# Column mean of an 8192 x 8192 float32 matrix: loads in float32 on SyncE's queue, sums in float32 in four column groups

## The chip, the cores and the metric

The kernel runs on one core of one Trainium2 chip. The metric is the device time of one execution in microseconds, taken as the median of several runs. A profiled execution gives the trace; its span runs from the first to the last instruction and is a little shorter than the time of a run.

## The reference

```python
def setup_inputs():
    return {
        "x": np.random.randn(8192, 8192).astype(np.float32),
    }

def reference(x: np.ndarray) -> np.ndarray:
    return np.mean(x, axis=0)
```

The input has 268.44 MB, all of which is read once; the output has 8192 float32 values (32 KB).

## The kernel before

**Tiling.** The 8192 rows are 64 slabs of 128 rows: a row of x lies along one SBUF partition, 8192 columns (32 KB of float32) long. Summing over the rows of a slab is a matrix product with a column of ones: `mm` (line 104) cuts a slab into 16 chunks of 512 columns, and `mm_seg` (line 90, the matmul at line 95) multiplies one chunk by `ones`, so that one output row of 512 sums is added up in PSUM over all 64 slabs. All matmuls are bf16, with a stationary operand of 128 x 1.

**Where the sums lie.** `acc` covers all eight PSUM banks. Chunks 0 to 7 are summed in partition 0, chunks 8 to 15 in partition 32, one chunk per bank; the last chunk is split into two halves of 256 columns, and its second half lies in partition 64 (`seg_psum`, line 82). These partitions decide which column group of TensorE a matmul uses.

**Loads.** Nearly all loads are issued on POOL's (GpSimd's) queue, and the transfer itself casts float32 to bf16, so half as many bytes are written to SBUF as are read:

- slab 0: its first 2048 columns come as float32 on SP's queue (`hx`, line 128) and are cast by VectorE (line 130); the rest comes over POOL (`t0`, line 136; the profile calls this buffer t_89).
- slabs 1 to 61: three slabs per transfer (line 158; 20 of them, 12.58 MB read and 6.29 MB written each), into two buffers; slab 61 comes alone (line 163). A load waits until TensorE has finished with the buffer.
- `place_orphans` (line 140): the last 8 rows of slab 62, columns 5632 to 8191, come early by a small load of their own (line 143) into the zeroed tile `xtra`, on partitions 0, 16, 32 and so on, and are added there.
- slab 62: two loads (lines 183 and 184), the second without those 8 rows.
- slab 63: pieces of 4096, 2048, 1024 and 512 columns (`b_piece`, line 200), then two of 256 (`b_cols`, line 223).

**Output.** `drain` (line 108) copies one row of 512 sums from PSUM to `res`, times 1/8192, alternately on VectorE (line 118) and ScalarE (line 116). `res` is one row on one partition, and goes out in four transfers: three on SP (lines 207, 213 and 237), one on ACT (line 240).

**Order.** Each queue runs in the order of the program. TensorE goes through the slabs in order; POOL issues loads ahead of it as far as the two slab buffers allow, and the tail's loads (lines 183 to 200), which have buffers of their own, right after the last slab load.

Of the kernel before, what the change touches and what calls it, by code (L numbers as in the profile page):

```python
# [7 lines left out]

@with_exitstack
def kernel(
# [8 lines left out]
    assert R % P == 0, "row count must be a multiple of 128"  # L21
    n_slabs = R // P
    s_last = n_slabs - 1

    MM_DT = mybir.dt.bfloat16
    CHUNK = 512
    BANKS = 8
    n_chunks = (C + CHUNK - 1) // CHUNK
    n_rows = (n_chunks + BANKS - 1) // BANKS + 1
    QROWS = (0, 32, 64, 96)  # L30
    assert n_rows <= len(QROWS)
    inv_r = 1.0 / float(R)

    SPD = int(os.environ.get("CM_SPD", "3"))
    HEADW = int(os.environ.get("CM_HEADW", "2048"))
    REB = int(os.environ.get("CM_REB", "1"))
    HEADW = min(HEADW, C)
    if HEADW % CHUNK:
        HEADW = (HEADW // CHUNK) * CHUNK

    two_slab_tail = n_slabs >= 4 and n_chunks == 16
    if not two_slab_tail or C < 2 * CHUNK:
        REB = 0
    DONOR_LO = 120
    ORPH_STEP = 16
    ORPHW = int(os.environ.get("CM_ORPHW", "2560"))
    ORPHW = min(max((ORPHW // CHUNK) * CHUNK, CHUNK), C)
    C1 = C - ORPHW

    const_pool = ctx.enter_context(tc.tile_pool(name="const", bufs=1))  # L50
    head_pool = ctx.enter_context(tc.tile_pool(name="head", bufs=1))
    slab_pool = ctx.enter_context(tc.tile_pool(name="slab", bufs=2))
    tail_pool = ctx.enter_context(tc.tile_pool(name="tail", bufs=1))
    psum_pool = ctx.enter_context(tc.tile_pool(name="acc", bufs=1, space=bass.MemoryType.PSUM))
    res_pool = ctx.enter_context(tc.tile_pool(name="res", bufs=1))

    ones_f32 = const_pool.tile([P, 1], mybir.dt.float32)
    nc.vector.memset(ones_f32, 1.0)
    ones = const_pool.tile([P, 1], MM_DT)
    nc.scalar.copy(out=ones, in_=ones_f32)  # L60

    if REB:
        xtra = tail_pool.tile([P, ORPHW], MM_DT, tag="xz")
        nc.vector.memset(xtra, 0.0)  # L64

    acc = psum_pool.tile([P, BANKS * CHUNK], mybir.dt.float32)
    res = res_pool.tile([1, C], mybir.dt.float32)

    def chunk_psum(c):
        q, b = c // BANKS, c % BANKS  # L70
        cw = min(CHUNK, C - c * CHUNK)
        return acc[QROWS[q] : QROWS[q] + 1, b * CHUNK : b * CHUNK + cw]

    FINW = CHUNK // 2

    def csegs(c):
        lo, hi = c * CHUNK, min(C, (c + 1) * CHUNK)
        if two_slab_tail and c == n_chunks - 1 and hi - lo == CHUNK:
            return ((lo, lo + FINW), (lo + FINW, hi))
        return ((lo, hi),)  # L80

    def seg_psum(c, lo, hi):
        q, b = c // BANKS, c % BANKS
        o = b * CHUNK - c * CHUNK
        if two_slab_tail and c == n_chunks - 1 and lo >= c * CHUNK + FINW:
            q += 1
            o = -(c * CHUNK + FINW)
        return acc[QROWS[q] : QROWS[q] + 1, o + lo : o + hi]

    def mm_seg(slab_ap, ordpos, c, lo, hi, base=0, prange=None):  # L90
        p0, p1 = (0, P) if prange is None else prange
        tp = None
        if prange is not None and p0 not in (0, 32, 64):
            tp = ((p0 // 32) * 32, QROWS[c // BANKS])
        nc.tensor.matmul(  # L95
            out=seg_psum(c, lo, hi),
            lhsT=ones[p0:p1, :],
            rhs=slab_ap[p0:p1, lo - base : hi - base],
            start=(ordpos == 0),
            stop=(ordpos == s_last),  # L100
            tile_position=tp,
        )

    def mm(slab_ap, ordpos, c, base=0, prange=None):
        for lo, hi in csegs(c):
            mm_seg(slab_ap, ordpos, c, lo, hi, base, prange)

    def drain(c, eng=None):
        c0 = c * CHUNK
        cw = min(CHUNK, C - c0)  # L110
        src_ap = chunk_psum(c)
        dst_ap = res[0:1, c0 : c0 + cw]
        if eng is None:
            eng = "dve" if c % 2 == 0 else "act"
        if eng == "act":
            nc.scalar.mul(out=dst_ap, in_=src_ap, mul=inv_r)  # L116
        else:
            nc.vector.tensor_scalar(  # L118
                out=dst_ap,
                in0=src_ap,  # L120
                scalar1=inv_r,
                scalar2=None,
                op0=mybir.AluOpType.mult,
            )

    if HEADW:
        hx = head_pool.tile([P, HEADW], mybir.dt.float32, tag="hx")
        nc.sync.dma_start(out=hx, in_=x[0:P, 0:HEADW])
        hxb = head_pool.tile([P, HEADW], MM_DT, tag="hxb")
        nc.vector.tensor_copy(out=hxb, in_=hx)  # L130
        for c in range(HEADW // CHUNK):
            mm(hxb, 0, c)

    if HEADW < C:
        t0 = slab_pool.tile([P, SPD * C], MM_DT, tag="slab")
        nc.gpsimd.dma_start(out=t0[:, : C - HEADW], in_=x[0:P, HEADW:C])  # L136
        for c in range(HEADW // CHUNK, n_chunks):
            mm(t0[:, : C - HEADW], 0, c, base=HEADW)

    def place_orphans():  # L140
        r0 = (n_slabs - 2) * P + DONOR_LO
        nd = P - DONOR_LO
        nc.gpsimd.dma_start(  # L143
            out=xtra.rearrange("(a b) c -> a b c", b=ORPH_STEP)[:nd, 0, :],
            in_=x[r0 : r0 + nd, C1:C],
        )
        for c in range(C1 // CHUNK, n_chunks):
            mm(xtra, 1, c, base=C1)

    bulk_end = (n_slabs - 2) if two_slab_tail else n_slabs  # L150
    s0 = 1
    first_group = True
    while s0 < bulk_end:
        ns = min(SPD, bulk_end - s0)
        slab = slab_pool.tile([P, SPD * C], MM_DT, tag="slab")
        src = x[s0 * P : (s0 + ns) * P, :]
        if ns > 1:
            nc.gpsimd.dma_start(  # L158
                out=slab[:, : ns * C].rearrange("p (k c) -> p k c", c=C),
                in_=src.rearrange("(k p) c -> p k c", p=P),  # L160
            )
        else:
            nc.gpsimd.dma_start(out=slab[:, :C], in_=src)  # L163
        for k in range(ns):
            for c in range(n_chunks):
                mm(slab[:, k * C : (k + 1) * C], s0 + k, c)
        s0 += ns
        if first_group:
            first_group = False
            if REB:  # L170
                place_orphans()

    if not two_slab_tail:
        for c in range(n_chunks):
            drain(c)
        nc.sync.dma_start(out=out[0:C], in_=res[0:1, 0:C])
        return

    sa = n_slabs - 2
    rowa = x[sa * P : (sa + 1) * P, :]  # L180
    abuf = tail_pool.tile([P, C], MM_DT, tag="ta")
    if REB:
        nc.gpsimd.dma_start(out=abuf[:, 0:C1], in_=rowa[:, 0:C1])  # L183
        nc.gpsimd.dma_start(out=abuf[0:DONOR_LO, C1:C], in_=rowa[0:DONOR_LO, C1:C])  # L184
        for c in range(n_chunks):
            if c < C1 // CHUNK:
                mm(abuf, sa, c)
            else:
                mm(abuf, sa, c, prange=(0, DONOR_LO))
    else:  # L190
        nc.gpsimd.dma_start(out=abuf, in_=rowa)
        for c in range(n_chunks):
            mm(abuf, sa, c)

    rowb = x[s_last * P : (s_last + 1) * P, :]
    bbuf = tail_pool.tile([P, C], MM_DT, tag="tb")

    def b_piece(c_lo, c_hi):
        lo, hi = c_lo * CHUNK, c_hi * CHUNK
        nc.gpsimd.dma_start(out=bbuf[:, lo:hi], in_=rowb[:, lo:hi])  # L200
        for c in range(c_lo, c_hi):
            mm(bbuf, s_last, c)

    b_piece(0, 8)
    for c in range(0, 8):
        drain(c)
    nc.sync.dma_start(out=out[0 : 8 * CHUNK], in_=res[0:1, 0 : 8 * CHUNK])

    b_piece(8, 12)
    drain(8, "dve"); drain(9, "act"); drain(10, "dve"); drain(11, "act")  # L210
    b_piece(12, 14)
    drain(12, "dve"); drain(13, "act")
    nc.sync.dma_start(out=out[8 * CHUNK : 14 * CHUNK], in_=res[0:1, 8 * CHUNK : 14 * CHUNK])
    b_piece(14, 15)
    drain(14, "dve")

    FIN = os.environ.get("CM_FIN", "act")
    lo15 = (n_chunks - 1) * CHUNK
    hi15 = min(C, lo15 + CHUNK)
    mid = lo15 + FINW  # L220

    def b_cols(lo, hi, eng):
        nc.gpsimd.dma_start(out=bbuf[:, lo:hi], in_=rowb[:, lo:hi])  # L223
        c = lo // CHUNK
        mm_seg(bbuf, s_last, c, lo, hi)
        src = seg_psum(c, lo, hi)
        dst = res[0:1, lo:hi]
        if eng == "act":
            nc.scalar.mul(out=dst, in_=src, mul=inv_r)  # L229
# [43 lines left out]
```

## Time and profile before

| | |
|---|---|
| median of 3 runs | 629.56 us (629.27 to 629.67) |
| span of the profiled execution | 627.5 us |
| DMA, mean of all engines over the span | 215 GB/s written; packets 9632, 134.91 MB |
| POOL's queue | 9472 packets, 133.70 MB (bf16) |
| SP's and ACT's queues | 152 packets, 1.08 MB |
| instruction loading | 8 packets, 0.13 MB |
| mean granted TensorE clock | 0.655 |

GB/s and the queues count the bytes that are written; the HBM row of the page counts what is read. The costliest groups of instructions (line, engine, operation, output and input, count; busy time and mean of one; idle time of the engine before them, and what ended it):

```
L95 PE MATMUL acc<-slab,ones 128*1 128x512 bf16 x1037 | 165.0, 439 | 426.3 <-DMA slab<-in_x_dram 426.3
L95 PEld LDWEIGHTS <-ones 128*1 128x1 bf16 x1094 | 63.3, 94 | 560.4 <-issue 513.4
L158 POOL DMA_DIRECT2D slab<-in_x_dram x20 | 15.3, 764 | 527.1 <-PE acc L95 527.1
L118 DVE TENSOR_SCALAR res<-acc 1x512 f32<-1x512 f32 x8 | 5.3, 678 | 613.1 <-PE acc L95 613.1
L116 ACT ACTIVATE res<-acc 1x512 f32<-1x512 f32 x7 | 3.9, 583 | 618.2 <-PE acc L95 618.2
```

An engine's idle time costs nothing where the engine is not the bound: TensorE waits 426.3 us for the slab loads, and POOL 527.1 us for TensorE to release a slab buffer.

### The profile page before, as it was taken

Reading aid. Unit: us, or ns where it says so; the run is one execution under the profiler, and the core shown is the slowest. Engines: PE = TensorE matmul, PEld = TensorE weight load, DVE = VectorE, ACT = ScalarE, POOL = GpSimd, SP = SyncE. Lnnn points to the kernel's source line nnn. Section 1 sums busy time; section 2 is a strip of 40 time slices with the busy share of each in tenths; the row PEclk is TensorE's granted clock in tenths of the full one; section 3 lists DMA queues with packets and bytes.
Section 4 is the critical chain, followed back from the end, with each engine's and each line's share of the span. In section 5 each row is a group of like instructions: output and inputs, shape, how many; then the busy total and the mean of one; then the engine's idle time right before and its main releaser. Section 6 shows DMA issues by size and latency. Waiting matters only on the chain.

```text
span 627.5 us, 2316 instructions
## 1 busy us (share of the span) xinstructions
PE 181.1 (29%) x1094; PEld 63.3 (10%) x1094; DVE 8.0 (1%) x12; ACT 5.7 (1%) x10; POOL 21.6 (3%) x35
## 2 busy tenths in 40 slices
PE   3032405040504133140405040422314050405165
PEld 0011101010101011010101010101101010101021
DVE  1000000000000000000000000000000000000003
ACT  0000000000000000000000000000000000000002
POOL 1000000000000000000000000000000000002000
PEclk9997666575757575656757575757566565757587
DMA  9999999999999999999999999999999999999997
GB/s 219 217 218 217 217 217 217 217 217 217 217 217 217 217 217 217 217 217 217 216 216 216 216 217 215 217 217 217 217 217 215 216 217 217 216 213 218 216 214 143
DMA packets 9632, 134.91 MB, mean 215 GB/s; under 512 B 532, under 2 KB 917, under 8 KB 1302
## 3 DMA queue, kind: packets, MB, share of 16 engines
q0 software_dynamic: 9472, 133.70, 100.0%
q1 hardware_dynamic: 150, 1.08, 0.5%
q8 instruction: 8, 0.13, 0.1%
q10 hardware_dynamic: 2, 0.00, 0.0%
HBM read 268.44 MB, written 0.03 MB: 428 GB/s over the span
## 4 chain that ended last, share of the span: by engine, by line
DMA 84%; PE 14%; issue 1%; POOL 0%; DVE 0%; DVEq 0%; POOLq 0%
DMA slab<-in_x_dram 77%; PE acc L95 14%; DMA bbuf<-in_x_dram 7%; DVE res L118 0%; POOL t_89 L136 0%; POOL slab L163 0%; POOL abuf L183 0%; POOL abuf L184 0%; DVEq L268 0%; POOLq L257 0%
## 5 line engine op out<-in xcount | busy, mean ns | idle before, releaser
L95 PE MATMUL acc<-slab,ones 128*1 128x512 bf16 x1037 | 165.0, 439 | 426.3 <-DMA slab<-in_x_dram 426.3
L95 PEld LDWEIGHTS <-ones 128*1 128x1 bf16 x1094 | 63.3, 94 | 560.4 <-issue 513.4
L158 POOL DMA_DIRECT2D slab<-in_x_dram x20 | 15.3, 764 | 527.1 <-PE acc L95 527.1
L118 DVE TENSOR_SCALAR res<-acc 1x512 f32<-1x512 f32 x8 | 5.3, 678 | 613.1 <-PE acc L95 613.1
L116 ACT ACTIVATE res<-acc 1x512 f32<-1x512 f32 x7 | 3.9, 583 | 618.2 <-PE acc L95 618.2
L95 PE MATMUL acc<-bbuf,ones 128*1 128x512 bf16 (+1 forms) x17 | 5.8, 599 | 3.3 <-DMA bbuf<-in_x_dram 3.3
L95 PE MATMUL acc<-abuf,ones 128*1 128x512 bf16 (+2 forms) x17 | 4.1, 517 | 2.9 <-DMA abuf<-in_x_dram 2.9
L95 PE MATMUL acc<-t_89,ones 128*1 128x512 bf16 (+1 forms) x13 | 3.4, 589 | 4.1 <-DMA t_89<-in_x_dram 4.1
L95 PE MATMUL acc<-hxb,ones 128*1 128x512 bf16 x4 | 1.9, 622 | 6.7 <-DVE hxb L130 6.7
L200 POOL DMA_DIRECT2D bbuf<-in_x_dram x4 | 2.1, 547 | 0.0
L223 POOL DMA_DIRECT2D bbuf<-in_x_dram x2 | 1.1, 532 | 26.0 <-DMA slab<-in_x_dram 26.0
L163 POOL DMA_DIRECT2D slab<-in_x_dram x1 | 0.6, 586 | 29.1 <-PE acc L95 29.1
L60 ACT ACT_TABLE_LOAD x1 | 1.3, 1283 | 0.7 <-PEq L257 0.7
L130 DVE CAST hxb<-hx 128x2048 bf16<-128x2048 f32 x1 | 1.2, 1227 | 3.2 <-DMA hx<-in_x_dram 3.2
L95 PE MATMUL acc<-xtra,ones 128*1 128x512 bf16 (+1 forms) x6 | 1.1, 343 | 0.0
L64 DVE MEMSET xtra<- 128x1280 uint32 x1 | 1.1, 1125 | 0.2 <-issue 0.2
L136 POOL DMA_DIRECT2D t_89<-in_x_dram x1 | 0.7, 669 | 0.8 <-POOLq L257 0.8
L143 POOL DMA_DIRECT2D xtra<-in_x_dram x1 | 0.6, 588 | 0.0
L184 POOL DMA_DIRECT2D abuf<-in_x_dram x1 | 0.6, 556 | 0.0
L183 POOL DMA_DIRECT2D abuf<-in_x_dram x1 | 0.6, 553 | 0.0
L231 DVE TENSOR_SCALAR res<-acc 1x256 f32<-1x256 f32 x1 | 0.4, 405 | 0.0
L229 ACT ACTIVATE res<-acc 1x256 f32<-1x256 f32 x1 | 0.4, 377 | 0.1
(6 smaller groups left out, 0.7 us busy)
## 6 DMA issues: line engine op xcount, KB each, us to landing
slab<-in_x_dram POOLq DMA_DIRECT2D x20, 6144.0 KB, 49.9
slab<-in_x_dram POOLq DMA_DIRECT2D x1, 2048.0 KB, 30.0
t_89<-in_x_dram POOLq DMA_DIRECT2D x1, 1536.0 KB, 11.4
abuf<-in_x_dram POOLq DMA_DIRECT2D x1, 1408.0 KB, 36.6
hx<-in_x_dram SPq DMA_DIRECT2D x1, 1024.0 KB, 4.7
bbuf<-in_x_dram POOLq DMA_DIRECT2D x1, 1024.0 KB, 42.9
abuf<-in_x_dram POOLq DMA_DIRECT2D x1, 600.0 KB, 38.6
bbuf<-in_x_dram POOLq DMA_DIRECT2D x1, 512.0 KB, 44.9
```

Source lines behind the costliest of these rows:

```text
L60: nc.scalar.copy(out=ones, in_=ones_f32)
L64: nc.vector.memset(xtra, 0.0)
L95: nc.tensor.matmul(out=seg_psum(c, lo, hi), lhsT=ones[p0:p1, :], rhs=slab_ap[p0:p1, lo - base : hi - base], start=(ordpos == 0), stop=(ord ...
L116: nc.scalar.mul(out=dst_ap, in_=src_ap, mul=inv_r)
L118: nc.vector.tensor_scalar(out=dst_ap, in0=src_ap, scalar1=inv_r, scalar2=None, op0=mybir.AluOpType.mult,)
L130: nc.vector.tensor_copy(out=hxb, in_=hx)
L136: nc.gpsimd.dma_start(out=t0[:, : C - HEADW], in_=x[0:P, HEADW:C])
L143: nc.gpsimd.dma_start(out=xtra.rearrange("(a b) c -> a b c", b=ORPH_STEP)[:nd, 0, :], in_=x[r0 : r0 + nd, C1:C],)
L158: nc.gpsimd.dma_start(out=slab[:, : ns * C].rearrange("p (k c) -> p k c", c=C), in_=src.rearrange("(k p) c -> p k c", p=P),)
L163: nc.gpsimd.dma_start(out=slab[:, :C], in_=src)
L200: nc.gpsimd.dma_start(out=bbuf[:, lo:hi], in_=rowb[:, lo:hi])
L223: nc.gpsimd.dma_start(out=bbuf[:, lo:hi], in_=rowb[:, lo:hi])
```

## The change

The kernel's body is written anew:

- **Loads.** All loads are plain float32 transfers on SP's queue, with no cast; POOL issues nothing. A tile is 256 rows: partition p holds rows 2p and 2p+1 of the tile, one run of 64 KB in memory. Three buffers of 64 KB per partition; 31 such tiles of 8.39 MB.
- **The last 256 rows** are the 32nd tile: first 128 rows in one transfer (32 KB per partition), then the last 128 rows in six pieces of 2048, 2048, 2048, 1024, 512 and 512 columns, each a transfer of its own.
- **Sums.** TensorE adds in float32. The columns are split into the same six pieces; each piece has one PSUM bank, and its four quarters are summed in partitions 0, 32, 64 and 96, in four column groups. The stationary operand `w` is 128 x 32, filled with 1/8192, so the mean comes out of the matmul itself and each group holds the same row 32 times.
- **Output.** Each piece is copied from PSUM with all 128 partitions, alternately by ScalarE and VectorE, and one row of each group is sent out: six transfers, alternately on ACT and SP, all after the last copy in the program.
- **Dropped:** the cast of hx, the tile of zeros and its orphan rows, the tail's own buffers, the multiplication by 1/8192 at the end, and the switches read from the environment.

```diff
+F32 = mybir.dt.float32
+PIECES = (2048, 2048, 2048, 1024, 512, 512)
+KROWS = 2
+BUFS = 3
...
-    ones_f32 = const_pool.tile([P, 1], mybir.dt.float32)
-    nc.vector.memset(ones_f32, 1.0)
-    ones = const_pool.tile([P, 1], MM_DT)
-    nc.scalar.copy(out=ones, in_=ones_f32)
+    NP = len(PIECES)
+    starts = [sum(PIECES[:i]) for i in range(NP)]
...
+    slab_pool = ctx.enter_context(tc.tile_pool(name="slab", bufs=BUFS))
...
+    w = const_pool.tile([P, 32], F32)
+    nc.vector.memset(w, 1.0 / R)
+
+    acc = [psum_pool.tile([P, 512], F32, name=f"acc{i}", tag=f"acc{i}") for i in range(NP)]
+    res = [
+        const_pool.tile([P, PIECES[i] // 4], F32, name=f"res{i}", tag=f"res{i}")
+        for i in range(NP)
+    ]
...
+    def piece_mm(ap, base, i, row):
+        n = PIECES[i] // 4
+        for q in range(4):
+            c0 = starts[i] + q * n - base
+            nc.tensor.matmul(
+                out=acc[i][32 * q : 32 * q + 32, 0:n],
+                lhsT=w,
+                rhs=ap[:, c0 : c0 + n],
+                start=(row == 0),
+                stop=(row == n_rows - 1),
+                tile_position=(0, 32 * q),
             )
...
+    row = 0
+    n_tiles = R // (KROWS * P)
+    for t in range(n_tiles - 1):
+        slab = slab_pool.tile([P, KROWS * C], F32, tag="slab")
+        src = x[t * KROWS * P : (t + 1) * KROWS * P, :]
+        nc.sync.dma_start(out=slab, in_=src.rearrange("(p k) c -> p (k c)", k=KROWS))
+        for k in range(KROWS):
+            for i in range(NP):
+                piece_mm(slab[:, k * C : (k + 1) * C], 0, i, row)
+            row += 1
...
+    last = slab_pool.tile([P, KROWS * C], F32, tag="slab")
+    r0 = (n_tiles - 1) * KROWS * P
+    for k in range(KROWS - 1):
+        nc.sync.dma_start(out=last[:, k * C : (k + 1) * C], in_=x[r0 + k * P : r0 + (k + 1) * P, :])
+        for i in range(NP):
+            piece_mm(last[:, k * C : (k + 1) * C], 0, i, row)
+        row += 1
+    off = (KROWS - 1) * C
+    for i in range(NP):
+        a, b = starts[i], starts[i] + PIECES[i]
+        nc.sync.dma_start(out=last[:, off + a : off + b], in_=x[R - P : R, a:b])
+    for i in range(NP):
+        piece_mm(last[:, off : off + C], 0, i, row)
+        n = PIECES[i] // 4
+        if i % 2 == 0:
+            nc.scalar.copy(out=res[i], in_=acc[i][:, 0:n])
+        else:
+            nc.vector.tensor_copy(out=res[i], in_=acc[i][:, 0:n])
+    for i in range(NP):
+        n = PIECES[i] // 4
+        a, b = starts[i], starts[i] + PIECES[i]
+        eng = nc.sync if i % 2 else nc.scalar
+        eng.dma_start(
+            out=out[a:b].rearrange("(q n) -> q n", q=4),
+            in_=res[i].rearrange("(q r) n -> q r n", r=32)[:, 0, :],
         )
```

In the text, a row of the changed kernel means one set of 128 input rows (`row` in the code): 64 in all, two to a tile, numbered 0 to 63.

More of the change, by code (lines that the diff above doesn't have):

```diff
@@ L1 @@
-import os
 from contextlib import ExitStack
@@ L20 @@
     R, C = x.shape
[L21 to L48, printed above, removed]
+    assert sum(PIECES) == C and R % (KROWS * P) == 0
+    NP = len(PIECES)
+    starts = [sum(PIECES[:i]) for i in range(NP)]
@@ L50 @@
     const_pool = ctx.enter_context(tc.tile_pool(name="const", bufs=1))
-    head_pool = ctx.enter_context(tc.tile_pool(name="head", bufs=1))
-    slab_pool = ctx.enter_context(tc.tile_pool(name="slab", bufs=2))
-    tail_pool = ctx.enter_context(tc.tile_pool(name="tail", bufs=1))
+    slab_pool = ctx.enter_context(tc.tile_pool(name="slab", bufs=BUFS))
     psum_pool = ctx.enter_context(tc.tile_pool(name="acc", bufs=1, space=bass.MemoryType.PSUM))
-    res_pool = ctx.enter_context(tc.tile_pool(name="res", bufs=1))
@@ L57 @@
-    ones_f32 = const_pool.tile([P, 1], mybir.dt.float32)
-    nc.vector.memset(ones_f32, 1.0)
-    ones = const_pool.tile([P, 1], MM_DT)
-    nc.scalar.copy(out=ones, in_=ones_f32)
[L62 to L101, printed above, removed]
-        )
@@ L104, in mm @@
[L104 to L229, printed above, removed]
-        else:
-            nc.vector.tensor_scalar(
-                out=dst, in0=src, scalar1=inv_r, scalar2=None,
-                op0=mybir.AluOpType.mult,
-            )
@@ L236 @@
-    b_cols(lo15, mid, "dve")
-    nc.sync.dma_start(out=out[14 * CHUNK : mid], in_=res[0:1, 14 * CHUNK : mid])
-    b_cols(mid, hi15, FIN)
-    if FIN == "act":
-        nc.scalar.dma_start(out=out[mid:C], in_=res[0:1, mid:C])
-    else:
-        nc.sync.dma_start(out=out[mid:C], in_=res[0:1, mid:C])
+    assert R & (R - 1) == 0
+    w = const_pool.tile([P, 32], F32)
[5 more added lines that the diff above has]
+    ]
@@ new lines @@
+    n_rows = R // P
+    seen = [0]
+    def piece_mm(ap, base, i, row):
[9 more added lines that the diff above has]
+                tile_position=(0, 32 * q),
+            )
+    row = 0
+    n_tiles = R // (KROWS * P)
```

## The prediction

> **What bounds the kernel now.** I read the page from the top: busy time first, then the DMA rows, then the chain of work that ended last.
>
> ```profile
> span 627.5 us, 2316 instructions
> PE 181.1 (29%) x1094; PEld 63.3 (10%) x1094; DVE 8.0 (1%) x12; ACT 5.7 (1%) x10; POOL 21.6 (3%) x35
> ...
> DMA  9999999999999999999999999999999999999997
> ...
> HBM read 268.44 MB, written 0.03 MB: 428 GB/s over the span
> ...
> DMA 84%; PE 14%; issue 1%; POOL 0%; DVE 0%; DVEq 0%; POOLq 0%
> ```
>
> Nothing computes for more than 29% of the span, the DMA engines are at 9 tenths in all slices but the last, and the chain is 84% DMA. The chain in order of time gives the period: it returns to the same point every two slabs.
>
> ```profile
> 399.85 49.32 DMA slab<-in_x_dram
> 449.18 0.04 issue
> 449.22 8.39 PE acc L95 x45
> 457.61 0.28 issue
> 457.89 49.31 DMA slab<-in_x_dram
> ```
>
> From 399.85 to 457.89 is 58.04 us for two slabs of 3 x 128 rows of 32 KB, 25.166 MB read: **433.6 GB/s**. The 8.39 us of PE lies between a landing and the next issue on POOL, but the other slab's load runs meanwhile: stretches of the trace between 51 and 574 us all show 217 GB/s written (bf16, half of what is read). So the read rate sets the time: 268.44 MB / 433.6 = 619.1 us of 627.5; the rest is start and end.
>
> The stretches of the start, the end, and one burst of PE (columns: from:to, length, busy of PE, PEld, DVE, ACT, POOL, granted clock, DMA share, GB/s written):
>
> ```profile
> 1.50:2.00 0.50, 0.00 (x0) 0.00 (x0) 0.50 (x1) 0.50 (x1) 0.50 (x2) 1.00 0.89 147
> 2.00:2.50 0.50, 0.00 (x0) 0.08 (x1) 0.24 (x1) 0.22 (x2) 0.50 (x1) 1.00 0.58 147
> 2.50:3.00 0.50, 0.00 (x0) 0.00 (x0) 0.00 (x0) 0.00 (x0) 0.50 (x2) 1.00 0.92 360
> 3.00:4.00 1.00, 0.00 (x0) 0.00 (x0) 0.00 (x0) 0.00 (x0) 0.23 (x1) 1.00 0.98 410
> ...
> 566.00:568.00 2.00, 2.00 (x9) 0.71 (x9) 0.00 (x0) 0.00 (x0) 0.00 (x0) 0.50 1.00 213
> 570.00:572.00 2.00, 2.00 (x23) 0.79 (x20) 0.00 (x0) 0.00 (x0) 0.00 (x0) 1.00 0.88 188
> ...
> 621.00:622.00 1.00, 1.00 (x6) 0.44 (x5) 0.82 (x2) 0.66 (x2) 0.00 (x0) 0.50 1.10 179
> 622.50:623.00 0.50, 0.50 (x2) 0.13 (x1) 0.50 (x1) 0.48 (x2) 0.00 (x0) 0.50 0.72 94
> ```
>
> **The stream (float32 into SBUF).** Bytes read stay the same; bytes written double, to as much as is read. The one float32 load of before, hx on SP's queue, shows what that costs: in 3.00:4.00 the engines wrote 410 GB/s, while casts alone never write over about 217. So the write side carries at least 410, and the upper bound is 268.44 MB / 410 = 654.7 us, +35.6. The lower bound: with the shorter runs at the end (10 to 22 KB in abuf) the trace wrote 209 between 600 and 615 us against 217, 3.7% less; if such a loss halved with each doubling of the run, 64 KB instead of 32 KB would gain about 1%, some 6 us. The steady row (32 KB, 433.6) is nearest to the new loads in size and run, so I stay by it and take a fifth of that gain, **-1.2**, with bounds of -6 and +35.6.
>
> Here the Trainium skill speaks against the change. "HBM Reference", section Specifications, puts a core streaming alone at about 425 GB/s; this trace shows 433.6. "DMA: Bandwidth & Descriptors", section on the iDMA fabric, has a load stream from SP at 408.7 GB/s (1 MiB per DMA, 4 KiB rows), which no run here shows. By 425 the stream would be an estimated 12.5 us longer, by 408.7 an estimated 38; I set both behind the row, since the loads here are 8 MB in much longer runs.
>
> **TensorE.** Before, a slab is 3 x 17 matmuls with one bf16 output row in group 0, 32 or 64. At clock 0.50 the weight loads step by 0.43 us, which is a 128x512 matmul, so 0.215 at clock 1.00; yet 570:572 shows 23 in 2.00 us, 0.087 each. Matmuls of different column groups overlap, about 2.5 deep, though the program puts the groups eight matmuls apart. After, a tile of two rows has 48 matmuls, 16,384 columns, 32 slots of 512, in four interleaved groups. No row prices a float32 matmul: from 1 bf16 matmul up to 9 (24 bits as three pieces of 8, on both operands); I take 4 (two pieces each). In four groups: 32 x 0.215 x 4 / 4 = 6.9 us, and some 2.3 for the 4.6 us that each burst starts at half clock: 9.2 us in the tile's 8.39 MB / 433.6 = 19.35. So **0** on the path, with 10 us of cover; at 9 it would be 17.8, still covered, though late at the end.
>
> "FP8 and Floating Point Precision", section TensorE Precision Notes, also counts four passes for true FP32; by it the sum stays as it is.
>
> **Buffers and queues.** POOL's 31 loads go, with their waits for PE; SP issues 31 tile loads, one row load and six pieces. A load waits until PE has finished the tile three back; behind it on SP stand the later loads and, after the last, three outputs. At a landing two further tiles (38.7 us of transfer) are issued, or one and a half under way; PE needs 9.2, so the queue never runs dry: **0**. If PE took over some 38 us the wait would show. The CAST of hx (1.23), the memset of xtra (1.12), the orphan load (40 KB) and 31 POOL issues all lay beside DMA: 0.
>
> **Start.** SP's first issue stays at 0.74. 1.50:2.50 wrote 147 where 3.00:4.00 wrote 410, some 0.6 us lost; a first load of 8 MB keeps the ramp but not the dip at share 0.58: **-0.3** (0 to -0.6).
>
> **End of the stream.** From 600 to 623.5 the stretches fall short of 217 by 1.65 us in sum (209, 205, 190, 189, 179, 139, 94). After, row 62 comes in 32 KB runs, and only row 63 in pieces of 8, 8, 8, 4, 2 and 2 KB runs; at 195 for its 4.19 MB it loses 1.1, and about 0.3 when it stops: **-0.3** (-1 to +1).
>
> **After the last landing.** Before: the last bbuf matmul is released at about 623.6, the span ends at 627.5: 3.9. After: four 128x128 matmuls on a warm PE, 0.22 plus latency, 0.5; hop 0.05; DVE copy of 128 elements (rows 1x512 678 ns, 1x256 405: 1.07 ns an element, 0.27); SP issue to the end as before, 625.45 to 627.5, 2.05: 2.9. ACT issues three outputs in a row behind its last copy, at 0.50 (its one issue before) to 0.23 (SP's): copy done 0.2 after the landing, 0.7 to 1.5 of issues, 1.8 to the end: 2.7 to 3.5. I take 3.3: **-0.6** (-1.2 to 0).
>
> **Instructions.** Loading 2316 of them moved 0.13 MB on the same engines. 1536 matmuls with a weight load each are some 3,100 instructions, +0.1 us; with four pairs each, 12,300, +1.3. I take **+0.3**.
>
> **Sum.** -1.2 - 0.3 - 0.3 - 0.6 + 0.3 = -2.1: span 625.4. The median of the runs lies 629.56 - 627.5 = 2.06 above the profiled span, so **627.5 us**.
>
> **Rivals.**
> 1. Slower: **the write side**. If 4 bytes written per 4 read cost even a little, every tile pays. The other terms are worth -0.9, so from 432.1 GB/s downwards (268.44 MB in 621.3 us) the kernel is slower by over 1.3 us. Halfway between the bounds, 422, it is 636.1 - 619.1 - 0.9 = +16.1: 645.7; at 410, 664. For it: 410 is the most seen written steadily. Against: hx ran while casts shared the engines, and DMA share there was only 0.98. Chance 0.28.
> 2. Slower: **TensorE late**. If the groups overlap two deep only, a tile takes 13.8 + 2.3 = 16.1 us, still under 19.35, but the tile before the last two rows ends 3.3 us before the last landing and two rows of 6.9 follow: PE ends 10.5 after it in place of 0.5, 637.5. With no overlap, 27.5 a tile, 32 of them after a first landing at 21.5: about 907. The burst at 570:572 speaks against both. Chance 0.08.
> 3. **No change**: the queue cuts the 64 KB runs, start and end gain nothing, the stream keeps 433.6: -0.6 + 0.3 gives 629.3. Chance 0.14.
>
> The forecast has 0.50, with its own range 624.5 to 628.3.
>
> **Numbers.** A measurement can tell about 0.2%, 1.3 us, from no change. Faster 0.48 (the forecast nearly whole), same 0.18 (rival 3 and 0.04 from the edges of the forecast and of rival 1), slower 0.34. The range goes from 624.5 to 642: left out are the slower part of rival 1 (about 0.13, rates under 424), the serial case of rival 2 (0.02) and 0.05 below.
>
> **What would show it.** Right: the tile landings 19.2 to 19.4 us apart, 433 GB/s or more written, PE idle for about half of each tile, PE ending under 1 us after the last landing. Rival 1: landings 19.5 us or more apart with PE idle and DMA at 9 tenths. Rival 2: PE busy without gaps and SP's loads waiting for PE. The prediction is wrong if the landing period leaves 19.2 to 19.45, or if the last output ends over 5 us after the last landing.

## The result and the profile after

The changed kernel takes 631.78 us (median of 6 runs, 631.66 to 632.38) against 629.65 for the kernel before (629.27 to 629.70): a ratio of 1.0036 with a 95% interval of 1.0026 to 1.0047. It is slower by 2.1 us; 627.5 was forecast. The direction is wrong. That the time lies in the stated range is luck: the range reached up to 642 mainly to leave room for rival 1, a slow write side, and that is not what happened.

The page of the profiled execution, span, busy engines, DMA and the shares of the chain:

```profile
span 629.9 us, 6278 instructions
PE 297.9 (47%) x3072; PEld 100.8 (16%) x3072; DVE 1.5 (0%) x4; ACT 2.7 (0%) x4; POOL 0.2 (0%) x4
...
DMA  9999999999999999999999999999999999999995
...
q1 hardware_dynamic: 5496, 268.45, 98.6%
q8 instruction: 24, 0.39, 0.2%
...
HBM read 268.44 MB, written 0.03 MB: 426 GB/s over the span
...
DMA 79%; PE 16%; another core or an unknown queue 3%; issue 0%; SPq 0%; DVE 0%
```

DMA is still the bound and TensorE is idle half the time. New is how much of TensorE's program is loaded: 24 packets of 16 KB on q8, where the kernel before had 8. TensorE ran 3072 matmuls and 3072 weight loads, so each of the 1536 float32 matmuls is two of each: 6144 instructions, 256 for each of the 24 packets and 64 bytes for each instruction.

The starts of TensorE's work on each tile (start, length, group; in brackets the idle time before and what ended it) show when the loads landed:

```profile
22.84 9.44 PE L52 MATMUL acc<-slab,w 128*32 128x512 f32 x96 [22.84 <-DMA slab<-in_x_dram]
43.32 9.44 PE L52 MATMUL acc<-slab,w 128*32 128x512 f32 x96 [11.05 <-DMA slab<-in_x_dram]
62.63 10.02 PE L52 MATMUL acc<-slab,w 128*32 128x512 f32 x96 [9.87 <-DMA slab<-in_x_dram]
...
217.23 9.53 PE L52 MATMUL acc<-slab,w 128*32 128x512 f32 x96 [10.37 <-DMA slab<-in_x_dram]
236.54 8.41 PE L52 MATMUL acc<-slab,w 128*32 128x512 f32 x96 [9.78 <-DMA slab<-in_x_dram]
257.24 9.99 PE L52 MATMUL acc<-slab,w 128*32 128x512 f32 x96 [12.29 <-DMA slab<-in_x_dram]
276.59 8.86 PE L52 MATMUL acc<-slab,w 128*32 128x512 f32 x96 [9.35 <-DMA slab<-in_x_dram]
```

Most tiles land 19.30 to 19.35 us apart, a little faster than the 19.35 of before. But three of them come late by 1.2 to 1.4 us: 43.32 is 20.48 after its predecessor, 257.24 is 20.70, and a third, at 471.16, is 20.69. They are eleven tiles apart, and what they lose is never made good.

The stretches of the end (from:to, length, busy of PE, PEld, DVE, ACT, POOL, granted clock, DMA share, GB/s) show the sum of it:

```profile
618.00:620.00 2.00, 2.00 (x40) 0.96 (x32) 0.00 (x0) 0.00 (x0) 0.00 (x0) 1.00 1.00 417
620.00:621.00 1.00, 0.62 (x8) 0.00 (x0) 0.00 (x0) 0.31 (x1) 0.00 (x0) 1.00 1.01 406
621.00:623.00 2.00, 1.07 (x8) 0.16 (x8) 0.69 (x1) 0.27 (x1) 0.00 (x0) 1.00 0.56 226
623.00:625.00 2.00, 1.39 (x16) 0.32 (x16) 0.00 (x0) 0.46 (x1) 0.00 (x0) 1.00 0.51 198
625.00:625.50 0.50, 0.45 (x12) 0.13 (x8) 0.12 (x1) 0.13 (x1) 0.00 (x0) 1.00 0.47 180
625.50:626.00 0.50, 0.30 (x8) 0.03 (x4) 0.31 (x1) 0.14 (x1) 0.00 (x0) 1.00 0.01 4
```

Up to 625.5 us DMA is busy to about a half, not to a tenth or to all: eight of sixteen engines have finished, and eight still work, for about four microseconds.

The trace's records of the completions say the same for each load. A load is counted complete in 16 steps. The Trainium skill, "DMA: Bandwidth & Descriptors", section "Why a DMA increments its semaphore by 16 and not by 1", explains them as one step from each DMA engine, posted when its own share has landed; the half share above agrees. The records do not name the engine. The 16 steps in us after the first of them, for five loads of the changed kernel:

```
first at   the 16 completions
 41.3      0.00 0.04 0.11 0.13 0.17 0.21 0.23 0.25 0.39 0.39 0.45 0.46 0.50 0.52 0.66 1.95
176.8      0.00 0.05 0.08 0.10 0.14 0.15 0.18 0.33 0.34 0.53 1.61 1.63 1.68 1.77 1.80 1.82
331.3      0.00 0.07 0.08 0.14 0.15 0.32 0.33 0.51 1.46 1.55 1.61 1.70 3.08 3.11 3.21 3.24
485.9      0.00 0.07 0.08 0.14 0.15 0.32 0.33 0.51 2.90 3.01 3.07 3.08 3.11 3.13 4.55 4.59
621.3      0.00 0.07 0.08 0.11 0.15 0.31 0.32 0.48 4.29 4.38 4.47 4.50 4.51 4.53 4.54 4.61
```

Eight engines stay together. The other eight fall back one after the other by about 1.45 us each, until all eight are one step late, then two, then three: 24 fallings back, and 24 pieces of 16 KB on q8. The two go together load by load. In the five loads shown the late engines have lost 1, 6, 12, 18 and 24 steps, and by the end of each of them 1, 6, 12, 18 and 24 of the packets on q8 have started. The 1st, 9th and 17th packets, at 34.2, 245.7 and 454.8 us, come in the loads that make the three late tiles. That gave the theory: **each piece of instructions fetched during the stream holds up one DMA engine by about 1.45 us, the pieces go round eight engines, and a load is as late as its latest engine.** TensorE uses 192 instructions (12 KB) per tile, so eight pieces last some eleven tiles (128 / 12 = 10.7): the distance of the late landings.

### The profile page after: what moved, and what is told of

It reads as the page before. It is cut to its first block, busy times and chain, and to the rows that moved or that the text cites. A ratio compares the mean times of both kernels' runs of the same rounds, so it can differ in the third digit from the quotient of the medians.

```text
span 629.9 us, 6278 instructions
## 1 busy us (share of the span) xinstructions
PE 297.9 (47%) x3072; PEld 100.8 (16%) x3072; DVE 1.5 (0%) x4; ACT 2.7 (0%) x4; POOL 0.2 (0%) x4
## 4 chain that ended last, share of the span: by engine, by line
DMA 79%; PE 16%; another core or an unknown queue 3%; issue 0%; SPq 0%; DVE 0%
DMA slab<-in_x_dram 76%; PE acc L52 16%; DMA last<-in_x_dram 3%; SPq L66 0%; DVE res L89 0%
## 5 line engine op out<-in xcount | busy, mean ns | idle before, releaser
L52 PE MATMUL acc<-slab,w 128*32 128x128 f32 (+2 forms) x2976 | 289.8, 554 | 326.2 <-DMA slab<-in_x_dram 326.2
L52 PEld LDWEIGHTS acc<-slab,w 128*32 128x32 f32 x2976 | 98.4, 126 | 517.3 <-DMA slab<-in_x_dram 311.4
L52 PE MATMUL acc<-last,w 128*32 128x512 f32 (+2 forms) x96 | 8.1, 456 | 2.4 <-DMA last<-in_x_dram 2.3
L87 ACT COPY res<-acc 128x512 f32<-128x512 f32 (+1 forms) x3 | 1.4, 479 | 622.7 <-PE acc L52 622.7
L52 PEld LDWEIGHTS acc<-last,w 128*32 128x32 f32 x96 | 2.4, 109 | 8.1 <-DMA last<-in_x_dram 6.1
L89 DVE COPY res<-acc 128x512 f32<-128x512 f32 (+2 forms) x3 | 1.4, 469 | 624.5 <-PE acc L52 624.5
```

Source lines behind the costliest of these rows:

```text
L52: nc.tensor.matmul(out=acc[i][32 * q : 32 * q + 32, 0:n], lhsT=w, rhs=ap[:, c0 : c0 + n], start=(row == 0), stop=(row == n_rows - 1), tile ...
L87: nc.scalar.copy(out=res[i], in_=acc[i][:, 0:n])
L89: nc.vector.tensor_copy(out=res[i], in_=acc[i][:, 0:n])
```

## The experiments

All expectations were set down before the runs. One table holds what the conclusions rest on; the last load is the last 512 columns, and "eighth" is its eighth completion of sixteen, by which the undisturbed engines are done (except in e2, where only seven engines are undisturbed, done at 623.60, and the eighth completion is a late engine's). Whose the 8 KB pieces are is shown for e2 alone. Span and completions are of the profiled execution, the time is the median; all in us.

```
                    pieces in the stream   last load       from last
kernel               16 KB    8 KB     eighth    last       to end    span     time
before                 8       0       622.71    623.60     3.89     627.5    629.65
changed               24       0       621.83    625.96     3.96     629.9    631.78
e1_few_pe              1       0       621.45    622.85     3.50     626.4    628.42
e2_more_dve           24      18       626.41    640.60     3.95     644.5    646.46
e3_dve_sums            0       2       622.74    623.55     5.37     628.9    630.34
e4_short_runs         24       1       623.22    627.44     3.72     631.2    632.49
e5_16_per_row         16       0       621.85    624.59     4.48     629.1    630.97
e7_dve_carry           0       1       622.54    623.77     5.22     629.0    631.07
e8_dve_bf16_tail       0       2       625.07    626.18     4.46     630.6    632.97
e10_quarter_pe         7       1       622.42    623.72     3.95     627.7    629.12
```

### Fewer TensorE instructions: e1_few_pe

```diff
         for k in range(KROWS):
-            for i in range(NP):
-                piece_mm(slab[:, k * C : (k + 1) * C], 0, i, row)
+            if t == 0:
+                for i in range(NP):
+                    piece_mm(slab[:, k * C : (k + 1) * C], 0, i, row)
             row += 1
```

> The sums of tiles 1 to 30 are left out; all loads, the last 256 rows and the outputs stay, so TensorE runs 384 matmul and weight-load instructions in place of 6144. Theory (each 16 KB piece of instructions that is fetched during the stream holds up one of eight DMA engines by about 1.45 us, and 24 pieces make three steps of it): at most 2 pieces are left, the 16 completions of the last loads lie within 0 to 1.5 us of each other in place of 4.6, and the time falls by 3.0 to 4.5 us, to 627.3 to 628.8. Rival (the eight late engines are slow by themselves, or because of float32 writes or the long runs): the spread stays near 4.6 us and the time at 631.8.

628.42 us, 0.9981 of before (0.9973 to 0.9990), 3.4 us under the changed kernel with the same loads; the last landing is 3.1 us earlier. One piece was fetched, and one engine of sixteen is late, by 1.6 us in the last load. The queue of the pieces and the stretches of the end:

```profile
q8 instruction: 1, 0.02, 0.0%
...
620.00:621.00 1.00, 1.00 (x16) 0.25 (x8) 0.02 (x1) 0.59 (x1) 0.00 (x0) 1.00 1.04 401
621.00:622.00 1.00, 1.00 (x16) 0.16 (x8) 0.68 (x1) 0.16 (x1) 0.00 (x0) 1.00 0.20 74
622.00:623.00 1.00, 0.79 (x20) 0.26 (x16) 0.42 (x1) 0.43 (x1) 0.00 (x0) 1.00 0.07 25
```

The DMA share no longer halves at 621; it falls to 0.07, about one engine of sixteen (0.0625). So the eight late engines are not slow by themselves, and neither the float32 writes nor the 64 KB runs make them late. This run alone leaves it open whether it is TensorE's instructions or its reading of SBUF.

### More instructions elsewhere: e2_more_dve

```diff
+    scr = const_pool.tile([P, 1], F32)
+    for _ in range(2304):
+        nc.vector.memset(scr, 0.0)
```

> The changed kernel with 2304 memsets of 128x1 on VectorE at the start, which nothing waits for; 9 more pieces of 16 KB of instructions, TensorE as before. Theory of the instruction fetches: 33 pieces in place of 24, and where they fall on the same eight engines, one step more: spread about 6 us, time 633.1 to 633.5; if VectorE's pieces fall on the other eight engines, those become late by one step and the time stays at 631.8, with the spread smaller. Rival (what TensorE does to the stream, by its reads or its releases): nothing changes, 631.8 and 4.6 us.

646.46 us, 1.0267 of before (1.0253 to 1.0281). That pieces of instructions alone make the kernel slower was right; the size was missed by a factor of ten, since the pieces are not spread over eight engines as was expected. The memsets read no data and nothing waits for them. The queues and the stretches of the end:

```profile
q8 instruction: 24, 0.39, 0.2%
q14 instruction: 19, 0.16, 0.1%
...
624.00:626.00 2.00, 2.00 (x40) 1.03 (x36) 0.00 (x0) 0.00 (x0) 0.00 (x0) 0.99 0.53 202
626.00:628.00 2.00, 2.00 (x24) 0.48 (x17) 0.00 (x0) 0.00 (x0) 0.00 (x0) 1.00 0.34 128
628.00:630.00 2.00, 1.50 (x32) 0.70 (x24) 0.00 (x0) 0.00 (x0) 0.00 (x0) 1.00 0.05 20
630.00:640.00 10.00, 7.35 (x84) 2.18 (x88) 0.74 (x2) 1.17 (x2) 0.00 (x0) 1.00 0.07 28
```

VectorE's program came in 8 KB pieces on another queue, 18 of them during the memsets (18 x 128 instructions are the 2304), and one engine took them all. It is none of TensorE's eight: seven engines are undisturbed, eight are late by TensorE's pieces, and the sixteenth is this one. In the last load 15 completions lie within 5.0 us and the sixteenth comes 17.7 us after the first: 17.7 / 18 = 0.98 us a piece. From 628 to 640 a single engine works (share 0.05 to 0.07) while the other fifteen have nothing left. 0.15 MB of instructions, 0.05% of the bytes, cost 14.7 us.

### The dose between: e5_16_per_row

```diff
+        tail = ap[:, 6144:8192].rearrange("p (b q n) -> p q b n", b=4, q=4)
+        for q in range(4):
+            mm(3, q, 0, 512, tail[:, q], row)
```

The last 2048 columns are summed by four matmuls of 512 columns in place of twelve smaller ones; the same columns are read.

> The changed kernel with 16 matmuls per 128 rows in place of 24 (the last 2048 columns share one PSUM bank and are drained together): 4,144 TensorE instructions, 16 pieces of 16 KB in place of 24, same columns and same loads. Theory of the instruction fetches: two of the three steps, spread 2.9 to 3.3 us, last landing 1.5 us earlier; the joint drain at the end gives back 0.3 to 0.5: 630.5 to 631.0. Rival (TensorE's reading of SBUF slows eight engines; the columns read are the same): spread 4.6, 631.8 to 632.2.

630.97 us, 1.0023 of before (1.0014 to 1.0032). 16 pieces, the spread of the last load 3.02 us, its last completion 1.37 us earlier than in the changed kernel. The share again halves at the end:

```profile
q8 instruction: 16, 0.26, 0.1%
...
620.00:621.00 1.00, 0.78 (x8) 0.00 (x0) 0.16 (x1) 0.00 (x0) 0.00 (x0) 1.00 1.06 428
621.00:622.00 1.00, 0.00 (x0) 0.00 (x0) 0.54 (x1) 0.00 (x0) 0.00 (x0) 1.00 0.62 250
622.00:623.00 1.00, 0.84 (x8) 0.16 (x8) 0.00 (x0) 0.00 (x0) 0.00 (x0) 1.00 0.52 209
623.00:624.00 1.00, 0.85 (x20) 0.38 (x16) 0.00 (x0) 0.58 (x1) 0.00 (x0) 1.00 0.53 205
624.00:625.00 1.00, 0.79 (x19) 0.31 (x16) 0.00 (x0) 0.00 (x0) 0.00 (x0) 1.00 0.08 29
```

Two steps in place of three, with TensorE reading every column as before: its reading of SBUF is not the cause.

### Length of the runs: e4_short_runs

```diff
-KROWS = 2
-BUFS = 3
+KROWS = 1
+BUFS = 6
```

> The changed kernel with one row per partition and load: 32 KB runs, six buffers; instructions as in the changed kernel. Theory (the fixed cost of a run): the undisturbed engines take 19.35 us for 8.39 MB, as before, in place of 19.32, so 0.5 to 1.3 us longer: 632.3 to 633.1, spread still 4.6 us. Rival (the gain comes from SP's queue, not from the run): 631.8.

632.49 us, 1.0045 of before (1.0031 to 1.0059), 0.7 us over the changed kernel. By the first completions of the loads, 4.19 MB take 9.682 us on the undisturbed engines, or 19.36 for 8.39 MB; the changed kernel has 19.33. So 32 KB runs cost about 0.2%, here with loads half as large and twice as many buffers; which of the three costs it was not separated. The spread stays (4.87).

### Sums on VectorE: e3_dve_sums, e7_dve_carry, e8_dve_bf16_tail

The next three compute the whole mean with hardly any TensorE instruction in the stream. The first adds all rows but the last in one SBUF buffer, over 32 KB runs:

```diff
-                piece_mm(slab[:, k * C : (k + 1) * C], 0, i, row)
+        elif 1 < t < n_rows - 2:
+            nc.vector.tensor_tensor(out=total, in0=total, in1=slab, op=mybir.AluOpType.add)
```

> The whole mean: VectorE adds rows 0 to 62 in float32 in SBUF, TensorE sums only that total and the last 128 rows (96 matmuls, 192 with weight loads). Loads of one 128-row slab in 32 KB runs, five buffers. Theory: no piece of instructions is fetched during the stream, completions within 1 us, last landing 4.5 us earlier but up to 1.0 later for the shorter runs: 627.3 to 628.5. VectorE needs 8.6 us for a slab (1.07 ns an element), under the 9.66 of its load. Rival (engines slow by themselves): 631.8 or more.

630.34 us, 1.0013 of before (1.0004 to 1.0022). The forecast of 627.3 to 628.5 was missed. The pieces did what was expected: no 16 KB piece in the stream and all completions within 0.94 us. The last landing came 2.4 us earlier than in the changed kernel, where 3.5 to 4.5 were expected. Another 1.4 us were lost behind it: VectorE's add of row 62 and TensorE's double work (total and row 63) end late, and 5.37 us lie between last landing and end in place of 3.96.

The second carries the total from tile to tile in the tile buffers, over 64 KB runs, and hands total and row 62 to TensorE in bf16:

```diff
+        if prev is not None:
+            nc.vector.tensor_tensor(out=slab[:, :C], in0=slab[:, :C], in1=prev[:, :C], op=ADD)
+        if t < n_tiles - 2:
+            nc.vector.tensor_tensor(out=slab[:, :C], in0=slab[:, :C], in1=slab[:, C:], op=ADD)
```

> The whole mean, with rows 0 to 61 added up in float32 by VectorE in the tile buffers (the total is carried from tile to tile), the total and row 62 handed to TensorE in bf16, row 63 in float32; loads as in the changed kernel, 64 KB runs. 192 to 200 TensorE instructions. Theory: no piece of instructions is fetched during the stream; completions within 1 us; last landing at 621.3 to 622.0, 3.9 to 4.5 us to the end, 627.3 to 628.5. Rival (VectorE's two adds per tile, 17.4 us of 19.3, let the queue run dry): landings more than 19.35 us apart, 630 or more.

631.07 us, 1.0021 of before (1.0013 to 1.0030): missed. The last landing is at 623.77, later than the 621.3 to 622.0 expected: a tile takes 19.35 us here, 0.7 us more over the stream than with 19.33, and one 8 KB piece cost another 0.65; and 5.22 us follow it, with VectorE's last add ending at 621.9 and ScalarE's copies and output issues in a row behind TensorE.

The third is the first with the last add written in bf16, and four buffers:

```diff
-        nc.vector.tensor_tensor(out=total[:, a:b], in0=total[:, a:b], in1=prev[:, a:b], op=mybir.AluOpType.add)
+        nc.vector.tensor_tensor(out=half[:, a:b], in0=total[:, a:b], in1=prev[:, a:b], op=mybir.AluOpType.add)
```

> The whole mean, as in the run with VectorE's sums over 32 KB runs, but VectorE's last add writes the total of rows 0 to 62 in bf16, so TensorE needs 48 bf16 matmuls with their weight loads fewer passes at the end (144 instructions); four buffers. Theory (that run lost its gain at the end, where TensorE ended 2.2 us after the last landing): last landing at 623.5 again, spread under 1 us, TensorE ends under 1 us after it, 628.4 to 629.2, below both kernels. Rival (the end is set by the copies and outputs, not by TensorE): 629.8 to 630.4.

632.97 us, 1.0056 of before (1.0042 to 1.0070): missed. The end became shorter (4.46), but the loads came 9.71 us apart in place of 9.68, and the last landing 2.6 us later. What of this is the fourth buffer and what the rest was not separated.

### Seven pieces: e10_quarter_pe

Loads, tail and outputs of the changed kernel; VectorE adds four rows into one, TensorE sums that one:

```diff
+        if t % 2:
+            nc.vector.tensor_tensor(out=slab[:, :C], in0=slab[:, :C], in1=prev[:, :C], op=mybir.AluOpType.add)
+        nc.vector.tensor_tensor(out=slab[:, :C], in0=slab[:, :C], in1=slab[:, C:], op=mybir.AluOpType.add)
+        if t % 2:
+            for i in range(NP):
+                piece_mm(slab[:, :C], 0, i, t - 1)
```

> The whole mean with the changed kernel's loads, tail and outputs; VectorE adds each pair of 64 KB-run tiles in place, four rows into one, and TensorE sums that one row in float32 as before, so it runs about 1,824 instructions, 7 pieces of 16 KB. Theory (the time is set by the latest engine, and seven pieces go to seven different engines): one step only, spread 1.4 to 1.8 us as with a single piece, last landing as in the run with a single piece, 622.9, or up to 1 us later if VectorE's work costs what it did in the run with the carried total: 628.3 to 629.6. Rival (the loss grows with the number of pieces): 7/24 of 4.6 us, 1.3 us, with the pieces in one engine more than once: spread 3 us or more and 629.8 or more.

629.12 us, 0.9994 of before (0.9985 to 1.0003), 2.7 us under the changed kernel and not to be told from the kernel before. Seven pieces of 16 KB came, and in the last load seven engines are 1.26 to 1.72 us behind the first. An eighth is 0.96 behind: it fell back in the load that follows an 8 KB packet at 493.6 us. The spread of 1.72 us is hardly more than the 1.59 of a single piece. The queues and the stretches of the end:

```profile
q8 instruction: 7, 0.11, 0.1%
...
q14 instruction: 2, 0.02, 0.0%
...
621.00:622.00 1.00, 0.71 (x8) 0.16 (x8) 0.00 (x0) 0.00 (x0) 0.00 (x0) 1.00 0.94 369
622.00:623.00 1.00, 0.83 (x12) 0.16 (x8) 0.00 (x0) 0.58 (x1) 0.00 (x0) 1.00 0.50 191
623.00:624.00 1.00, 0.79 (x20) 0.32 (x16) 0.42 (x1) 0.27 (x2) 0.00 (x0) 1.00 0.11 43
```

One of the two packets on q14 falls into the stream. The time follows the number of pieces that the worst engine gets, not their sum. No version that computes the whole mean beat the kernel before by more than its interval.

## Why the prediction was wrong

With the eighth completion of the last load as the mark, the 2.4 us between the two spans part into three: the undisturbed engines, 621.83 against 622.71, **-0.9**; the late ones behind them, 4.13 against 0.89, **+3.2**; from the last landing to the end, 3.96 against 3.89, **+0.1**.

- **The bound** was read rightly: the stream, in both kernels.
- **The stream, the start and its end** were put at -1.2 - 0.3 - 0.3 = -1.8 and measured -0.9. The stream gave -0.6 (19.33 against 19.35 us a tile; e4 was 0.7 us slower). The start gave nothing in place of -0.3: the eighth completion of the first 4.19 MB came at 12.51 us before, that of the first 8.39 MB at 22.24 after; less 9.67 and 19.33 of transfer, 2.84 against 2.91. The last completions, at 12.63 and 22.70, give 3.0 against 3.4. What is left for the end is about -0.3, as forecast, though the 1.65 us that it was worked out from leave out the stretch 623.0 to 623.5 of before (16 GB/s, another 0.46). The bound of 410 GB/s on the write side was far too low: 8.39 MB in 19.33 us are 434.0. That casts alone never write over about 217 holds only for longer stretches: between 12 and 16 us two of 2 us show 254 and 262. The 434.0 lie also above the two rates of the Trainium skill that spoke against the change ("HBM Reference", section Specifications: about 425; "DMA: Bandwidth & Descriptors", section on the iDMA fabric: 408.7).
- **TensorE** was right: 8.4 to 10.0 us a tile against 9.2 forecast, four groups side by side, two matmuls of twice the bf16 length (the weight loads step by 0.85 us at clock 0.50) for each float32 one, so the factor of 4. The DMA engines never ran dry for it: the first completions of the 64 KB loads lie 19.30 to 19.37 us apart.
- **Instructions: this is the step that failed.** It was priced as bytes at the rate of the whole stream, that is, spread over all sixteen engines: 0.13 MB before, up to 1.3 us more, +0.3 taken. The count lay within its bounds (6,144). But a piece goes through one engine, holds it up by 1.45 us, and only eight engines are used, so 24 pieces are three steps on the latest engine and not 24/16 of a short transfer. Measured: +3.2. e1, e5 and e10 (1, 16 and 7 pieces) and e2 (18 pieces on one engine) show it.
- **After the last landing** -0.6 was forecast and +0.1 came. The mis-sized term is the time from SP's last issue to the end: taken over from before as 2.05 us, it measured 3.10 (626.82 to 629.92). Of the 1.1 us more, 0.27 is the issue itself, here of four partitions (0.50 us in place of 0.23), 0.14 the time from there to its landing, and 0.65 the time from the last landing of an output to the end of the span (1.53 in place of 0.88). What makes that last part longer is not shown; it is 1.46 to 1.54 us in the five runs whose trace has an 8 KB piece of instructions starting in the last 0.25 us of the span, and 0.88 to 1.08 in the five others. The issues of the changed kernel's output (engine, operation, count, duration in ns: least, median, most):

```profile
L94 ACTq DMA_DIRECT2D out_dram<-res x3: 514/520/1071, 621.3 to 626.2; - x3
L94 SPq DMA_DIRECT2D out_dram<-res x3: 500/513/657, 622.9 to 626.8; - x3
```

**The rivals.** None of the three is what happened. Rival 1 needed a stream under 432.1 GB/s; undisturbed it is 434.0. The landing period was named as the sign, and it nearly passes: most tiles lie in 19.2 to 19.45, and the cost sits in the three that do not. What the list lacked is an engine that falls behind the others.

## What to carry to other kernels

In a kernel whose DMA engines never rest, as here, instructions are traffic that is not spread: count the pieces that the program needs during the stream and divide by the engines that they go to, not by sixteen (here eight for TensorE's, at about 1.45 us a piece, and one for VectorE's in e2, at 0.98). Read the DMA share at the very end: a half or a sixteenth there means that some engines are behind, and a landing that is late once in many equal ones shows when they fell back. A cheaper instruction stream can be worth more than a faster transfer, even where TensorE has half its time free: handing it fewer rows (e10) was worth 2.7 us and wider matmuls (e5) 0.8, the longer runs in larger loads (e4) 0.7.

## What was not expected of the hardware

- A 16 KB piece of TensorE's program delays its engine by about 1.45 us, though its own packet is recorded as 0.88 to 0.97 us in the changed kernel; an 8 KB piece of VectorE's by 0.98, with packets of 0.31 to 0.33. What takes the rest is open, and so is which eight engines serve TensorE.
- All 18 of VectorE's pieces went through one engine, while TensorE's went round eight.
- In the kernel before, eight pieces made the one step that it has. There it is 0.89 us from the eighth completion to the last, against 1.40 for the one step of e1, with packets of 0.89 to 0.97 us in both; why it is smaller beside the casting loads is open. Its orphan rows let one engine finish its last load 3.3 us ahead of the eighth; that one was not among the late ones.
- Loads with 64 KB runs came 19.35 us apart in e7, where VectorE added without much pause, and 19.33 in the changed kernel; in e8, with four buffers, loads with 32 KB runs came 9.71 apart and not 9.68. What makes these differences is open.
